# Attention and retention products as three products of halves in a hybrid encoder trunk

## The chip, the cores and the metric

The kernel runs on one core of one Trainium2 chip. The metric is the device time of one execution in microseconds, from its start to its end, here the median of several runs of the same kernel. The profile comes from one further execution, whose own time stands beside its span below.

## What is computed

The reference is a two-layer encoder trunk, applied to 16 meta tokens, 256 prompt frames and 32 frames of a running stream with 512 cached frames. The kernel puts the three side by side as 304 columns (T), with channels on the partitions, so that every dense layer is one product over 304 columns, or 288 in the second layer, where the meta columns are no longer needed (c0 = 16). What matters here, cut to its core:

```python
def retention(q, k, v, s0):              # 4 heads, 128 key and 256 value channels
    def step(s, xs):                     # chunks of 64 frames
        qc, kc, vc = xs
        att = einsum('blhk,bmhk->bhlm', qc, kc) * d_intra
        o = einsum('bhlm,bmhv->blhv', att, vc) + einsum('blhk,bhkv->blhv', qc, s) * d_q
        ...
def stick_breaking(q, k_all, v_all, q_start):    # 8 heads of 128 channels
        z = einsum('bqhd,bshd->bhqs', qblk, k_all) * scale
        log_stay = where(visible, log_sigmoid(-z), 0.0)
        later = cumsum(log_stay, axis=3, reverse=True) - log_stay
        w = where(visible, exp(log_sigmoid(z) + later), 0.0)
        return einsum('bhqs,bshd->bqhd', w, v_all)
```

A layer is: a SwiGLU feed-forward block, layer norm, one wide input product (w_in) that makes queries, keys and values of retention and attention, a pooling branch and gates, three branches merged by the gates, an output product, layer norm, a second feed-forward block and layer norm.

## The kernel before, in words

**Halves.** The dense products are not run in plain f32. Every operand x is cut into hi, which is x rounded to the type f32r by a copy on ScalarE (`act`), and lo = x - hi, also f32r, by a subtraction on VectorE; `split` (L397) does both, and `split_t` (L429) does it into two fresh buffers of 304 columns. A product is then the sum of three f32r products: hi by hi, hi by lo, lo by hi. `dense` (L359) does so for eight or 22 tiles of 128 x 128 weights in L367 to L369. The weights come from HBM in blocks of 8 tiles (512 KB) over SyncE's queue, are cut by `prep_hi` (L237) and `prep_lo` (L243), three blocks (AHEAD) before TensorE uses them, and prep_lo puts out the fetch of the block five further on (NRAW). Outside dense, retention's second product (L922 to L927) uses halves too. The scores of retention (L888 to L890), the attention's scores (L733, L734) and its prompt values (L761, L762) are plain f32 products.

**Order of the work.** The program is written out by hand: every engine runs its instructions in the order in which the code puts them out (manual_schedule). TensorE's backbone is the sequence of dense calls. Beside it, generators in the list `side` are advanced by `pump` by one step, up to their next yield, at the start of each dense call; then `tick` runs functions that were put off by `defer` for so many calls; then come the dense product's matmuls; at its end `advance` continues epilogues that are open (stages). `settle` runs all of these to their end. One dense call of eight tiles is 24 matmuls.

**Attention.** The heads are done in two groups of four (g = 0, 1). For each group, 12 dense calls make keys (ks), values (vs) and queries (qs). The first 16 of the layer's 24 calls run on un, the activations before the norm's scale is known; their epilogues (`Norm.value`, L592) correct them with VectorE and GpSimd, and a copy on ScalarE follows one call later. `v_transposes` (L702) turns the values by TensorE and copies them from PSUM into vt. Four calls after group 0's last one (in the first one after group 1's), `sb_tasks` (L1116) settles and appends the generator `sb_group` (L722) to side. Its steps: scores(0); scores(1); the running stream's scores against the cache; turn(0) and scores(2); turn(1) and scores(3); turns of the stream's weights; turn(2); the stream's values and turn(3); two more turns; values(0) and values(1); values(2) and values(3). In `scores` (L731) two products, 144 columns for the first block of 128 queries and 272 for the second, go into one PSUM bank; ScalarE takes two sigmoids of it, VectorE a scan (L740), GpSimd and VectorE products. In `turn` (L747) three transposes bring the weights of one head into PSUM and one copy brings them to wt. `values` (L758) multiplies them with vt. Group 0's generator runs beside group 1's dense calls, group 1's beside the dense calls of retention's queries and keys, whose epilogue `rotary` (L853) needs three VectorE operations a call.

**Retention.** `ret_all` (L981) starts one head, `ret_head` (L883), every two turns, beside 24 dense calls. A head's first step has its three score products and three transposes, and the VectorE work on them; the second step splits the decayed scores; the third has the products with values; the later ones the head's norm. Each of the 24 calls advances every open head by one step.

**Buffers.** Large operands of 4 x 306 columns (`newquad`, L181) share 20 buffers; buffers of 304 columns (`t304`) 16; of 576 columns (`t560`) 7; PSUM has 8 banks. A buffer is taken where its first instruction stands, and that instruction waits until the last reader of the one before is done. While the groups start, un (four large buffers, hi and lo), hn (the normed activations in halves, four more, used by the calls from the 17th on) and x (the residual, two) are in use beside the groups' own; a call of the first 16 is called a chunk, 0 to 15, so that group 1 begins with chunk 12.

Of the kernel before, what the change touches and what calls it, by code (L numbers as in the profile page):

```python
# [11 lines left out]
F32R = mybir.dt.float32r  # L12
# [11 lines left out]
T = MP + SMP  # L24
# [144 lines left out]
def trunk(ctx, tc, xT, wts, kc_d, vc_d, s0_d, sp_d, vec_d, tab_d, y_d, kv_d, ret_d, pool_d):  # L169
# [11 lines left out]
    def newquad(name, dt=F32):  # L181
        return quad.tile([128, 4, TW], dt, tag="q", name=name)
# [11 lines left out]
    def t560(name, dt=F32):  # L194
        return tmp.tile([128, 576], dt, tag="w", name=name, bufs=NT_W)

    def pa():
        return ps8.tile([128, 512], F32, tag="p", name="pa")
# [10 lines left out]
    def act(out, in_, f=AF.Copy, **kw):  # L209
        A.activation(out, in_, f, **kw)  # L210
# [96 lines left out]
    side = []  # L307
# [89 lines left out]
    def split(hi, lo, src, e=None):  # L397
        act(hi, src)
        tt(e or V, lo, src, hi.bitcast(F32), ALU.subtract)
# [33 lines left out]
        return hi, lo  # L433


    def mean(i, parts, c):
        p = pa()
        PE.matmul(p[:, c], onesr[:, i], parts[0], start=True, stop=False)
        PE.matmul(p[:, c], onesr[:, i], parts[1], start=False, stop=True)
        return p  # L440
# [256 lines left out]
    def flat(q):  # L697
        return q.rearrange("p a b -> p (a b)")
# [3 lines left out]
    def v_transposes(vs, i, vt, vm):  # L702
        p = pa()
        for k in range(4):
            o = 16 + 128 * (k % 2)
            PE.transpose(p[:, k * 128:k * 128 + 128], vs[:, i - 1 + k // 2, o:o + 128], ident)
        act(flat(vt)[:, (i - 1) * 256:(i + 1) * 256], p)
        if i == 3:
            few = t304("few")[:, 0:256]
            for k, o in enumerate((0, 272)):  # L710
                act(few[:, k * 128:k * 128 + 128].rearrange("p (a b) -> p a b", a=4), vs[:, :, o:o + 32])
            defer(3, lambda: few_transposes(few, vm))
# [9 lines left out]
    def sb_group(l, g, c0, ks, qs, kc, vc, vt, vm, oh, ol):  # L722
        meta = c0 == 0
        W = 416
        wts_t = newquad("wt")
        wt = [flat(wts_t)[:, i * 384:i * 384 + 384] for i in range(3)]
        Ys = {}
        y2 = ym[g]
        rev = lambda a: a[:, W - 1::-1]

        def scores(i):  # L731
            pz = pa()
            PE.matmul(pz[:, 0:144], qs[:, i, 16:144], ks[:, i, 0:144], start=True, stop=True)  # L733
            PE.matmul(pz[:, 144:416], qs[:, i, 144:272], ks[:, i, 0:272], start=True, stop=True)  # L734
            X, Y = t560("X"), t560("Y")
            act(X[:, 0:W], pz[:, 0:W], AF.Sigmoid, scale=-SCALE)
            act(Y[:, 0:W], pz[:, 0:W], AF.Sigmoid, scale=SCALE)
            for o in (16, 288):
                tt(G, Y[:, o:o + 128], Y[:, o:o + 128], TB("low"), ALU.mult)
            V.tensor_tensor_scan(out=rev(X), data0=rev(X), data1=rev(TB("d1p")), initial=1.0,  # L740
                                 op0=ALU.mult, op1=ALU.max)
            two = lambda a, o: a[:, o:o + 288].rearrange("p (a b) -> p a b", a=2)[:, :, 0:16]
            tt(V, y2[:, :, i, 0:16], two(Y, 0), two(X, 1), ALU.mult)
            tt(V, Y[:, 16:W - 1], Y[:, 16:W - 1], X[:, 17:W], ALU.mult)
            Ys[i] = Y

        def turn(i):  # L747
            Y = Ys.pop(i)
            p = pa()
            for k, o in enumerate((16, 160, 288)):  # L750
                PE.transpose(p[:, k * 128:k * 128 + 128], Y[:, o:o + 128], ident)  # L751
            if i == 3:
                wt.append(t560("wt3")[:, 0:384])
            act(wt[i], p[:, 0:384])

        po = []

        def values(i):  # L758
            po.append(pa())
            v = flat(vt)[:, i * 256:i * 256 + 256]  # L760
            PE.matmul(po[i][:, 0:256], v[:, 0:128], wt[i][:, 0:256], start=True, stop=False)  # L761
            PE.matmul(po[i][:, 128:256], v[:, 128:256], wt[i][:, 256:384], start=False, stop=False)  # L762

        Ws = 560 if meta else 544
        scores(0)
        yield
        scores(1)
# [115 lines left out]
    def ret_head(l, c0, h, qr, kr, vt, s0, od, var):  # L883
        vh, vl = [flat(vt[k][h // 2])[:, (h % 2) * 512:(h % 2) * 512 + 512] for k in range(2)]
        vc = flat(vt[2])[:, h * 256:h * 256 + 256]
        p, pk = pa(), pa()
        q, k = qr[:, h], kr[:, h]
        PE.matmul(p[:, c0:272], k[:, 0:128], q[:, c0:272], start=True, stop=True)  # L888
        PE.matmul(p[:, 272:416], k[:, 128:256], q[:, 128:272], start=True, stop=True)
        PE.matmul(p[:, 416:464], k[:, T - 128:T], q[:, 256:304], start=True, stop=True)  # L890
        PE.transpose(pk[:, 0:128], k[:, 0:128], ident)
        PE.transpose(pk[:, 128:256], k[:, 128:256], ident)
        PE.transpose(pk[:, 256:384], k[:, T - 128:T], ident)
# [163 lines left out]
    with tc.manual_schedule():  # L1057
# [10 lines left out]
        for l in range(DEPTH):  # L1068
# [5 lines left out]
            for g in range(2):  # L1074
                kc, vc = sb_load(l, g)
                ks, vs, qs = newquad("ks"), newquad("vs"), newquad("qs")
                vt = newquad("vt")
                vm = tmp.tile([128, 256], F32, tag="vm", name="vm")

                def k_epi(i, ks=ks, g=g):  # L1080
# [34 lines left out]

                def sb_tasks(g=g, ks=ks, qs=qs, kc=kc, vc=vc, vt=vt, vm=vm):  # L1116
                    settle()
                    side.append(sb_group(l, g, c0, ks, qs, kc, vc, vt, vm, oh[g], ol[g]))

                defer(4 - 3 * g, sb_tasks)  # L1120

# [116 lines left out]
```

## Time and profile before

| | |
|---|---|
| median of 3 runs | 1759.21 us (1758.84 to 1759.56) |
| the profiled execution's own time | 1759.8 us |
| its span | 1758.0 us |
| TensorE (PE) busy | 1748.0 us, 12736 matmuls |
| VectorE (DVE) busy | 1081.0 us |
| ScalarE (ACT) busy | 855.1 us |
| GpSimd (POOL) busy | 512.6 us |
| TensorE's granted clock | 0.999 of 2.4 GHz |

In the profile, L12 is line 12 of the kernel and pd<-hnh,whi means that the instruction writes pd and reads hnh and whi. PE's matmuls are pipelined: a row's duration holds the latency, and two matmuls overlap, so that the distance from one start to the next is the time that one takes from the engine. SP and SPq are SyncE and its queue of DMA issues. A line such as L204 or L210 is that of a helper, and the names tell which use it is. A timeline row may join several instructions of one line ("x2").

### The profile page before, as it was taken

Reading aid. Unit: us, or ns where it says so; the run is one execution under the profiler, and the core shown is the slowest. Engines: PE = TensorE matmul, PEld = TensorE weight load, DVE = VectorE, ACT = ScalarE, POOL = GpSimd, SP = SyncE. Lnnn points to the kernel's source line nnn. Section 1 sums busy time; section 2 is a strip of 40 time slices with the busy share of each in tenths; the row PEclk is TensorE's granted clock in tenths of the full one; section 3 lists DMA queues with packets and bytes.
Section 4 is the critical chain, followed back from the end, with each engine's and each line's share of the span. In section 5 each row is a group of like instructions: output and inputs, shape, how many; then the busy total and the mean of one; then the engine's idle time right before and its main releaser. Section 6 shows DMA issues by size and latency. Waiting matters only on the chain.

```text
span 1758.0 us, 31540 instructions
## 1 busy us (share of the span) xinstructions
PE 1748.0 (99%) x12736; PEld 1734.2 (99%) x12736; DVE 1081.0 (61%) x1496; ACT 855.1 (49%) x1379; POOL 512.6 (29%) x494
## 2 busy tenths in 40 slices
PE   9999999999999999999999999999999999999998
PEld 9999999999999999999999999999999999999997
DVE  5444567655785669844578445676557846796444
ACT  5444456443554446544455444475446544565442
POOL 1111336210152236411335113362101421472111
PEclk9999999999999999999999999999999999999999
DMA  7545456344345444554445544564444555446551
GB/s 286 156 156 156 156 199 218 122 149 133 119 153 181 153 148 144 172 155 160 154 140 168 157 156 156 194 230 126 153 141 127 158 183 166 147 149 189 167 166 54
DMA packets 81634, 281.18 MB, mean 160 GB/s; under 512 B 8656, under 2 KB 15440, under 8 KB 81360
## 3 DMA queue, kind: packets, MB, share of 16 engines
q1 hardware_dynamic: 80576, 276.75, 49.5%
q8 instruction: 100, 1.64, 0.4%
q0 software_dynamic: 640, 2.10, 0.3%
q14 instruction: 46, 0.38, 0.1%
q10 hardware_dynamic: 272, 0.31, 0.1%
HBM read 270.62 MB, written 8.50 MB: 159 GB/s over the span
## 4 chain that ended last, share of the span: by engine, by line
PE 99%; DMA 0%; DVE 0%; ACT 0%; issue 0%; SPq 0%; ACTq 0%
PE pd L367 30%; PE pd L368 30%; PE pd L369 30%; PE pd L387 1%; PE pd L385 1%; PE pd L386 1%; PE pa L923 0%; PE pa L734 0%; PE pa L927 0%; PE pa L761 0%; DMA raw<-in_wts 0%; PE pa L751 0%; PE pa L928 0%; PE pa L812 0%; PE pa L772 0%; PE pa L733 0%
## 5 line engine op out<-in xcount | busy, mean ns | idle before, releaser
L204 DVE TENSOR_TENSOR wlo<-raw,whi 128x1024 fp32r<-128x1024 f32 (+1 forms) x493 | 634.5, 1289 | 267.3 <-issue 140.0
L210 ACT ACTIVATE whi<-raw 128x1024 fp32r<-128x1024 f32 (+1 forms) x493 | 515.5, 1051 | 178.1 <-PE pd L368 125.3
L367 PE MATMUL pd<-hnh,whi 128*128 128x304 f32 (+1 forms) x1696 | 517.4, 305 | 0.0
L368 PE MATMUL pd<-hnl,whi 128*128 128x304 f32 (+1 forms) x1696 | 510.3, 301 | 0.0
L369 PE MATMUL pd<-hnh,wlo 128*128 128x304 f32 (+1 forms) x1696 | 509.0, 300 | 0.0
L368 PEld LDWEIGHTS pd<-hnl,whi 128*128 128x128 f32 x1696 | 320.5, 189 | 0.6
L367 PEld LDWEIGHTS pd<-hnh,whi 128*128 128x128 f32 x1696 | 319.7, 189 | 0.7
L369 PEld LDWEIGHTS pd<-hnh,wlo 128*128 128x128 f32 x1696 | 320.2, 189 | 0.0
L367 PE MATMUL pd<-sh,whi 128*128 128x304 f32 (+1 forms) x704 | 212.0, 301 | 0.0
L369 PE MATMUL pd<-sh,wlo 128*128 128x304 f32 (+1 forms) x704 | 211.9, 301 | 0.0
L368 PE MATMUL pd<-sl,whi 128*128 128x304 f32 (+1 forms) x704 | 211.9, 301 | 0.0
L204 POOL TENSOR_TENSOR sl<-sg,sh 128x304 fp32r<-128x304 f32 (+1 forms) x64 | 75.4, 1178 | 344.3 <-ACT sh L210 338.8
L367 PE MATMUL pd<-unh,whi 128*128 128x306 f32 (+1 forms) x520 | 157.5, 303 | 0.0
L368 PE MATMUL pd<-unl,whi 128*128 128x306 f32 (+1 forms) x520 | 157.1, 302 | 0.0
L369 PE MATMUL pd<-unh,wlo 128*128 128x306 f32 (+1 forms) x520 | 156.7, 301 | 0.0
L204 POOL TENSOR_TENSOR un<-un,rs_y 128x304 f32<-128x304 f32 (+1 forms) x80 | 100.2, 1260 | 146.9 <-DVE cc L595 120.5
L367 PEld LDWEIGHTS pd<-sh,whi 128*128 128x128 f32 x704 | 132.9, 189 | 0.0
L369 PEld LDWEIGHTS pd<-sh,wlo 128*128 128x128 f32 x704 | 132.8, 189 | 0.0
L368 PEld LDWEIGHTS pd<-sl,whi 128*128 128x128 f32 x704 | 132.8, 189 | 0.0
L210 ACT ACTIVATE sh<-sg 128x304 fp32r<-128x304 f32 (+1 forms) x88 | 39.9, 456 | 186.5 <-DVE sg L204 148.5
L204 DVE TENSOR_TENSOR sg<-sg,pd 128x304 f32<-128x304 f32 (+1 forms) x64 | 29.8, 466 | 122.5 <-PE pd L369 120.9
L368 PEld LDWEIGHTS pd<-unl,whi 128*128 128x128 f32 x520 | 98.3, 189 | 0.0
(286 smaller groups left out, 3160.6 us busy)
## 6 DMA issues: line engine op xcount, KB each, us to landing
raw<-in_wts SPq DMA_DIRECT2D x491, 512.0 KB, 3.6
kc<-in_kc SPq DMA_DIRECT2D x8, 512.0 KB, 5.8
vc<-in_vc SPq DMA_DIRECT2D x8, 512.0 KB, 6.8
out_kv<-ks SPq DMA_DIRECT2D x4, 608.0 KB, 5.5
out_kv<-vs SPq DMA_DIRECT2D x4, 608.0 KB, 6.0
out_ret<-st POOLq DMA_DIRECT2D x8, 256.0 KB, 2.3
tab<-in_tab SPq DMA_DIRECT2D x1, 1753.0 KB, 8.7
out_y<-x SPq DMA_DIRECT2D x4, 288.0 KB, 2.3
```

Of the source, the lines that this page charges most:

```text
L204: e.tensor_tensor(out=out, in0=a, in1=b, op=op)
L210: A.activation(out, in_, f, **kw)
L367: PE.matmul(o, wh, xh[:, c0:c1], start=(k == 0), stop=False)
L368: PE.matmul(o, wh, xl[:, c0:c1], start=False, stop=False)
L369: PE.matmul(o, wl, xh[:, c0:c1], start=False, stop=(k == n - 1))
L385: PE.matmul(o, wh, xh[:, c0:c1], start=(k == 0), stop=False)
L386: PE.matmul(o, wh, xl[:, c0:c1], start=False, stop=False)
L387: PE.matmul(o, wl, xh[:, c0:c1], start=False, stop=(k == len(xs) - 1))
```

## The change

A helper `mm3` runs a product as the three products of halves, and `cut` takes a range of columns of both halves. The attention's scores run on halves of queries and keys that `halves(i)` makes by two split_t calls: halves(0) before the generator's first yield, to which sb_tasks now advances it at once, and halves(i + 1) within scores(i), after its products. The values of the prompt (vt) and the weights (wt) become pairs: where one copy on ScalarE brought them from PSUM, split now does, with one more VectorE subtraction. The pairs take two large buffers in place of one each; the fourth head's weights take two buffers of 576 columns in place of one. In ret_head, keys and queries are split in a step of their own, ahead of the scores, so that every head has one step more. The products over cached frames, the stream's own and the meta tokens' stay as they were.

```diff
@@ -433,6 +433,15 @@
         return hi, lo
 
 
+    def mm3(out, w, x, start=True, stop=True):
+        for i, (a, b) in enumerate(((0, 0), (0, 1), (1, 0))):
+            PE.matmul(out, w[a], x[b], start=start and i == 0, stop=stop and i == 2)
+
+
+    def cut(hl, a, b):
+        return [x[:, a:b] for x in hl]
+
+
     def mean(i, parts, c):
         p = pa()
         PE.matmul(p[:, c], onesr[:, i], parts[0], start=True, stop=False)
@@ -704,7 +713,7 @@
         for k in range(4):
             o = 16 + 128 * (k % 2)
             PE.transpose(p[:, k * 128:k * 128 + 128], vs[:, i - 1 + k // 2, o:o + 128], ident)
-        act(flat(vt)[:, (i - 1) * 256:(i + 1) * 256], p)
+        split(*[flat(v)[:, (i - 1) * 256:(i + 1) * 256] for v in vt], p)
         if i == 3:
             few = t304("few")[:, 0:256]
             for k, o in enumerate((0, 272)):
@@ -722,16 +731,24 @@
     def sb_group(l, g, c0, ks, qs, kc, vc, vt, vm, oh, ol):
         meta = c0 == 0
         W = 416
-        wts_t = newquad("wt")
-        wt = [flat(wts_t)[:, i * 384:i * 384 + 384] for i in range(3)]
+        wts_t = [newquad("wth", F32R), newquad("wtl", F32R)]
+        wt = [[flat(w)[:, i * 384:i * 384 + 384] for w in wts_t] for i in range(3)]
         Ys = {}
         y2 = ym[g]
         rev = lambda a: a[:, W - 1::-1]
 
+        qk = {}
+
+        def halves(i):
+            qk[i] = split_t(qs[:, i, 16:272]), split_t(ks[:, i, 0:272])
+
         def scores(i):
+            q, k = qk.pop(i)
             pz = pa()
-            PE.matmul(pz[:, 0:144], qs[:, i, 16:144], ks[:, i, 0:144], start=True, stop=True)
-            PE.matmul(pz[:, 144:416], qs[:, i, 144:272], ks[:, i, 0:272], start=True, stop=True)
+            mm3(pz[:, 0:144], cut(q, 0, 128), cut(k, 0, 144))
+            mm3(pz[:, 144:416], cut(q, 128, 256), k)
+            if i < 3:
+                halves(i + 1)
             X, Y = t560("X"), t560("Y")
             act(X[:, 0:W], pz[:, 0:W], AF.Sigmoid, scale=-SCALE)
             act(Y[:, 0:W], pz[:, 0:W], AF.Sigmoid, scale=SCALE)
@@ -750,18 +767,20 @@
             for k, o in enumerate((16, 160, 288)):
                 PE.transpose(p[:, k * 128:k * 128 + 128], Y[:, o:o + 128], ident)
             if i == 3:
-                wt.append(t560("wt3")[:, 0:384])
-            act(wt[i], p[:, 0:384])
+                wt.append([t560(n, F32R)[:, 0:384] for n in ("wt3h", "wt3l")])
+            split(*wt[i], p[:, 0:384])
 
         po = []
 
         def values(i):
             po.append(pa())
-            v = flat(vt)[:, i * 256:i * 256 + 256]
-            PE.matmul(po[i][:, 0:256], v[:, 0:128], wt[i][:, 0:256], start=True, stop=False)
-            PE.matmul(po[i][:, 128:256], v[:, 128:256], wt[i][:, 256:384], start=False, stop=False)
+            v = [flat(x)[:, i * 256:i * 256 + 256] for x in vt]
+            mm3(po[i][:, 0:256], cut(v, 0, 128), cut(wt[i], 0, 256), stop=False)
+            mm3(po[i][:, 128:256], cut(v, 128, 256), cut(wt[i], 256, 384), start=False, stop=False)
 
         Ws = 560 if meta else 544
+        halves(0)
+        yield
         scores(0)
         yield
         scores(1)
@@ -883,11 +902,13 @@
     def ret_head(l, c0, h, qr, kr, vt, s0, od, var):
         vh, vl = [flat(vt[k][h // 2])[:, (h % 2) * 512:(h % 2) * 512 + 512] for k in range(2)]
         vc = flat(vt[2])[:, h * 256:h * 256 + 256]
+        q, k = qr[:, h], kr[:, h]
+        kh, qh = split_t(k[:, 0:T]), split_t(q[:, c0:T])
+        yield
         p, pk = pa(), pa()
-        q, k = qr[:, h], kr[:, h]
-        PE.matmul(p[:, c0:272], k[:, 0:128], q[:, c0:272], start=True, stop=True)
-        PE.matmul(p[:, 272:416], k[:, 128:256], q[:, 128:272], start=True, stop=True)
-        PE.matmul(p[:, 416:464], k[:, T - 128:T], q[:, 256:304], start=True, stop=True)
+        mm3(p[:, c0:272], cut(kh, 0, 128), cut(qh, 0, 272 - c0))
+        mm3(p[:, 272:416], cut(kh, 128, 256), cut(qh, 128 - c0, 272 - c0))
+        mm3(p[:, 416:464], cut(kh, T - 128, T), cut(qh, 256 - c0, T - c0))
         PE.transpose(pk[:, 0:128], k[:, 0:128], ident)
         PE.transpose(pk[:, 128:256], k[:, 128:256], ident)
         PE.transpose(pk[:, 256:384], k[:, T - 128:T], ident)
@@ -1074,7 +1095,7 @@
             for g in range(2):
                 kc, vc = sb_load(l, g)
                 ks, vs, qs = newquad("ks"), newquad("vs"), newquad("qs")
-                vt = newquad("vt")
+                vt = [newquad("vth", F32R), newquad("vtl", F32R)]
                 vm = tmp.tile([128, 256], F32, tag="vm", name="vm")
 
                 def k_epi(i, ks=ks, g=g):
@@ -1115,7 +1136,9 @@
 
                 def sb_tasks(g=g, ks=ks, qs=qs, kc=kc, vc=vc, vt=vt, vm=vm):
                     settle()
-                    side.append(sb_group(l, g, c0, ks, qs, kc, vc, vt, vm, oh[g], ol[g]))
+                    gen = sb_group(l, g, c0, ks, qs, kc, vc, vt, vm, oh[g], ol[g])
+                    next(gen)
+                    side.append(gen)
 
                 defer(4 - 3 * g, sb_tasks)
 
```

## Rows read from the trace of the kernel before

**Rows 1.** The page: busy time, share and instructions; chain that ended last.

```profile
PE 1748.0 (99%) x12736; PEld 1734.2 (99%) x12736; DVE 1081.0 (61%) x1496; ACT 855.1 (49%) x1379; POOL 512.6 (29%) x494
...
PE 99%; DMA 0%; DVE 0%; ACT 0%; issue 0%; SPq 0%; ACTq 0%
```

**Rows 2.** Waits of PE: waited for, us in total, times, longest.

```profile
PE pa L271 <- POOL onesr L1059: 1.1, 1, 1.1
```

**Rows 3.** PE's timeline, attention: start us, us, line, operands, shapes, xcount.

```profile
331.67 0.60 PE L761 MATMUL pa<-wt,vt 128*128 128x256 f32 x2
332.10 0.38 PE L762 MATMUL pa<-wt,vt 128*128 128x128 f32 x2
332.32 0.41 PE L733 MATMUL pa<-ks,qs 128*128 128x144 f32 x2
332.57 0.62 PE L734 MATMUL pa<-ks,qs 128*128 128x272 f32 x2
332.83 0.51 PE L367 MATMUL pd<-hnh,whi 128*128 128x304 f32 x1
333.17 0.30 PE L368 MATMUL pd<-hnl,whi 128*128 128x304 f32 x1
333.31 0.30 PE L369 MATMUL pd<-hnh,wlo 128*128 128x304 f32 x1
```

**Rows 4.** PE's timeline, scores and transposes of a retention head.

```profile
422.05 0.62 PE L888 MATMUL pa<-qr,kr 128*128 128x272 f32 x2
422.50 0.41 PE L889 MATMUL pa<-qr,kr 128*128 128x144 f32 x2
422.75 0.32 PE L890 MATMUL pa<-qr,kr 128*128 128x48 f32 x2
422.90 0.29 PE L891 MATMUL pa<-tab,kr 128*128 128x128 f32 x1
423.03 0.27 PE L892 MATMUL pa<-tab,kr 128*128 128x128 f32 x1
423.14 0.27 PE L893 MATMUL pa<-tab,kr 128*128 128x128 f32 x1
```

**Rows 5.** PE's timeline, retention: narrow f32 (L924) and wide f32r products (L927).

```profile
430.55 0.30 PE L924 MATMUL pa<-qd,s 128*128 128x32 f32 x2
430.69 0.37 PE L927 MATMUL pa<-xbh,vtrh 128*128 128x272 f32 x1
430.90 0.29 PE L927 MATMUL pa<-xbl,vtrh 128*128 128x272 f32 x1
431.02 0.29 PE L927 MATMUL pa<-xbh,vtrl 128*128 128x272 f32 x1
431.15 0.46 PE L928 MATMUL pa<-xc,vtrc 128*128 128x176 f32 x2
```

**Rows 6.** Tile st_hi: a split's copy and subtraction; ns min/median/max.

```profile
L210 ACT ACTIVATE st_hi<-rsm x8: 444/451/457, 434.2 to 1344.7; 128x304 fp32r<-128x304 f32 x4, 128x288 fp32r<-128x288 f32 x4
L204 DVE TENSOR_TENSOR st_lo<-rsm,st_hi x8: 458/468/480, 434.7 to 1345.2; 128x304 fp32r<-128x304 f32 x4, 128x288 fp32r<-128x288 f32 x4
```

**Rows 7.** ACT's timeline, last key copies before scores(0), both layers; [idle before].

```profile
286.88 0.55 ACT L210 ACTIVATE ks<-un,cc 128x304 f32<-128x304 f32 x1 [2.32 <-POOL un L204]
...
1168.17 0.55 ACT L210 ACTIVATE ks<-un,cc 128x304 f32<-128x304 f32 x1 [2.32 <-POOL un L204]
```

**Rows 8.** PE's timeline: scores(0), group 0, both layers; scores(3), group 1, first layer.

```profile
287.32 0.41 PE L733 MATMUL pa<-ks,qs 128*128 128x144 f32 x2
...
347.83 0.41 PE L733 MATMUL pa<-ks,qs 128*128 128x144 f32 x2
...
1168.23 0.41 PE L733 MATMUL pa<-ks,qs 128*128 128x144 f32 x2
```

**Rows 9.** Waits of SyncE's queue: us in total, times, longest.

```profile
SPq L693 <- DMA out_kv<-vs: 1.6, 2, 0.9
```

**Rows 10.** DVE's timeline: last rotary products ahead of group 1's third scan.

```profile
345.12 0.96 DVE L204 TENSOR_TENSOR rt<-pd,tab 64x304 f32<-64x304 f32 x2
```

## Prediction

> **What bounds the kernel now.** I read the page's busy shares and the chain that ended last first: TensorE (PE) is busy for 99% of the span and the chain is PE for 99% of it [rows 1]. The reader is to see that any PE time that a change adds or removes goes one for one into the span. Next the view of waits, for PE alone: the longest is 1.1 us, for the first constants, before the work begins [rows 2]. So in the attention and retention stages PE waits for nobody; the other engines run ahead of it and have slack, but no queue is free of order: each works through its own program, and what stands behind a late instruction is late too. Then I read PE's timeline at the products that change, since durations of pipelined matmuls overlap and only the distance of starts is a price.
>
> The sum is made against the profiled execution, 1758.0 us of span in a run of 1759.8 us; the median of the runs is 1759.21, 0.6 below it, and the forecast is the median plus the sum. About 0.2% (3.5 us) is what a measurement of this kernel can tell from no change.
>
> **Prices of the products.** A plain f32 product appears as two records. For one attention head the two score products of 144 and 272 columns cost 0.25 us (332.32 to 332.57) and 0.46 us (332.57 to the start of L368 at 333.17, less the 0.14 of the dense product between), so 0.71; the value products of 256 and 128 columns cost 0.43 and 0.22, so 0.65 [rows 3]. For one retention head L888 to L890 cost 0.45, 0.25 and 0.15, with 0.02 more between the first two transposes than between the next: 0.87 [rows 4]; the second layer has 256 columns in place of 272 there and I take 0.85.
>
> What one f32r product costs is seen only for wide ones: 272 columns start 0.125 us after one another (430.90, 431.02, 431.15) and 304 columns 0.14 [rows 3, 5], that is 0.46 ns a column: 0.118 us for 256 columns. The new products of 144, 128 and 48 columns have no row. By the column they would be 0.066, 0.059 and 0.022 us; at the price of f32 they would be 0.25, 0.22 and 0.15. The nearest row is L924 with 32 columns: from the first of its two records to the start of the second L927 are 0.35 us (430.55 to 430.90), of which the first L927 streams for 0.125, so each 32-column record took 0.11 though its columns are a quarter of that [rows 5]. I read this as the time to load 128 columns of weights, a floor that the next product, an f32r one, paid too. I take 0.112 for every f32r product under 240 columns, and keep the column price and the f32 price as ends.
>
> **The change on PE.** Each product becomes three, hi by hi, hi by lo, lo by hi. Scores, 16 heads over both layers: 3 x 0.112 + 3 x 0.125 = 0.71, as before. Values: 3 x 0.118 + 3 x 0.112 = 0.69, 0.035 more, 0.6 us in all. Retention, 8 heads: 3 x 0.125 + 6 x 0.112 = 1.05 (1.03 in the second layer), 0.175 more, 1.4 us in all. Sum on PE: **+2.0 us**.
>
> The Trainium skill ("FP8 and Floating Point Precision", TensorE Precision Notes) gives full f32 four passes through the array; three passes for four would take a quarter off the 16 x 1.36 + 8 x 0.86 = 28.6 us of these products, 7.2 us. The rows bear out the four passes for wide products (0.46 us for 272 columns against 0.125 for one f32r pass); they also show the load that narrow products don't outrun, and that turns the gain into a small loss.
>
> **The change on the other engines.** It adds to every attention head two splits ahead of the scores (256 and 272 columns) and to every retention head two of 304 or 288, each one copy on ScalarE and one subtraction on VectorE; those of 304 columns take 0.45 and 0.47 us [rows 6]. Where weights and values were copied, the copy stays and a subtraction is added. Together some 20 us on ScalarE and 35 us on VectorE. As a load PE covers that: weights are split three blocks, 10 us, ahead. What counts is who waits behind whom.
>
> First, the head start of each group. Its halves(0) is put out in the tick after settle(), and the next dense call begins with scores(0): a distance of one dense product, 3.4 us. For the first group of each layer settle() ends with a copy of keys that on ScalarE runs at 286.88, after 2.32 us of waiting for GpSimd, and for 0.55 us; in the second layer at 1168.17 [rows 7]. PE starts those scores at 287.32 and 1168.23 [rows 8]. Before, the scores didn't need that copy; now the two hi copies (0.40 and 0.42, from the 304-column price) stand behind it, and the last lo ends 0.42 later: 287.43 + 0.82 + 0.42 = 288.7 and 1170.0. PE can do the first of six products meanwhile (0.11), so it waits 1.3 and 1.65 us: 2.95. Behind the waiting VectorE subtraction stands one weight block, needed 10 us later.
>
> Added to it: the 20 large buffers. When the second group loads its caches, the four un, the four hn, one x, and the first group's two kc, two vc, ks, qs and vt are alive, 16, and the four loads make 20; the last load waits for the DMA out of the old values in both layers [rows 9]. With vt in two halves the count is 21, so a later user, the first copy of keys, must wait until the product of chunk 15 is half through (about 285.6). ScalarE loses about 3 us, of which the 2.32 us of idling give most back; I bound the cost between 0 and 0.9 us a layer and take 0.45, **+3.9 us** with the former. SyncE's queue is held up to 6 us as well, with weight fetches behind it, which are issued some 13 us before ScalarE needs them.
>
> Second, scores(3) of the second group of each layer. There VectorE also has the rotary products: it ends one at 346.08 and has the scan next, while PE reaches scores(3) at 347.83 [rows 8, 10]. Two splits added in the steps before delay it by 0.85 to 1.7 (the lower end where its waits for GpSimd absorb one), then come the lo half of the weights, 384 columns, 0.59, and those of halves(3), 0.82: done at 348.3 to 349.2. PE waits 0.4 to 1.25 us, I take 0.7 in each layer: **+1.4 us**. The first group has no rotary work beside it, and I cost its later splits at nothing; without that idle VectorE time it would pay the same 0.7.
>
> Retention: halves go out one turn, 3.4 us, ahead of the products, and later heads have the products of the head before between; nothing. The chain of the heads ends one turn later, with some six turns to spare before the drain. Its cover gone, it would cost one turn's splits, 1.8 us.
>
> Sum: 2.0 + 3.9 + 1.4 = 7.3, so 1766.5 us (1767.1 for the profiled execution's own time).
>
> **The rivals.** *Narrow f32r products cost what f32 ones do.* No row speaks for it but that none narrower than 256 columns is f32r now. Each of the three then costs 0.25, 0.22 or 0.15: 16 x (3 x 0.138 + 3 x 0.108) + 8 x (3 x 0.138 + 3 x 0.038) = 16 us more, 1782. Chance 0.14.
>
> *The waits don't come*, because ScalarE and VectorE get to the halves earlier than the keys' copy lets me think. Against it stands the program's order on ScalarE. 1761.2, within 0.2%. Chance 0.11.
>
> *The load is hidden*, so narrow products run at the column price: 48 x 0.046 + 48 x 0.053 + 24 x 0.046 + 24 x 0.09 = 8.0 us less than the forecast, 1758.5: not slower. It decides from a distance of starts under 0.086 us (8.0 us over 144 narrow products is 0.055 each; 3.8 us, which bring it within 0.2%, are 0.026 each). L924 speaks against it [rows 5]. The Trainium skill ("TensorE: Matmul & The Clock Gate", Back-to-back issue gap) gives pairs of load and matmul about 81 ns at 128 columns; by that the time would be some 4.5 us under the forecast, 1762. No row here comes that low. Chance 0.11. Both this and the former together: 1753, chance 0.04.
>
> **How the numbers follow.** Forecast 0.60, of which 0.05 ends within 0.2%; its own range is 1762 to 1770.5 (waits of 3.75 to 7.25 us, narrow products between 0.09 and 0.125). Slower by over 0.2%: 0.55 + 0.14 = 0.69. Within: 0.05 + 0.11 + 0.08 of the hidden load = 0.24. Faster: 0.04 + 0.03 = 0.07. The range 1758 to 1772 takes in all but the f32 price and the case of both, 0.18, and some 0.02 for waits that I don't see.
>
> **What would show it.** In the profile after: starts of the 144-column f32r products 0.11 us apart and of the 48-column ones too (0.02 would be the hidden load, 0.15 to 0.25 the f32 price); L734's successor, L761's and L888's totals of 0.71, 0.69 and 1.05 us a head; among PE's waits, four in all of note, two for a st_lo half at about 287.4 and 1168.3, of 1.3 to 2.2 us, and two under 1.3 us near 348 and 1227; the first copy of keys on ScalarE in the second group after, not before, the middle of chunk 15. PE waits in the retention stage, or for weights, would prove me wrong, and so would a time under 1762.

## The result, and the profile after

The changed kernel takes 1772.39 us (median of 6 runs, 1771.03 to 1773.76) against 1759.38 us for the kernel before (6 runs, 1758.64 to 1760.22): a ratio of 1.0072, 95% interval 1.0062 to 1.0083, or 13.0 us more. The forecast was 1766.5, with a range of 1758 to 1772, and the result lies 0.4 us beyond its upper end. The profiled execution, the fastest of the six, took 1771.03 us, with a span of 1769.3, 11.3 more than before.

Page of the kernel after: busy time, and the chain that ended last.

```profile
PE 1752.8 (99%) x12824; PEld 1741.1 (98%) x12824; DVE 1112.7 (63%) x1568; ACT 870.0 (49%) x1427; POOL 507.2 (29%) x494
...
PE 92%; DVE 3%; POOL 2%; ACT 1%; issue 1%; DMA 0%; SPq 0%; ACTq 0%; DVEq 0%; POOLq 0%
```

The shares of busy time hardly move, and in PE's row of the page, rounded to tenths of a slice, nothing is to be seen. The chain says it: it was PE for 99% [rows 1], and now 8% of it passes through the other engines. Waits of PE after (us in total, times, longest), which answer to [rows 2]:

```profile
PE pa L438 <- ACT st_hi L210: 4.5, 2, 2.4
PE pa L438 <- DVE st_lo L204: 2.3, 4, 1.2
PE pa L271 <- POOL onesr L1080: 1.1, 1, 1.1
```

L438 is the product in mm3. PE's timeline at three of its waits, first and second layer (idle time and what ended it in brackets):

```profile
288.73 0.33 PE L438 MATMUL pa<-st_hi 128*128 128x144 f32 x1 [2.08 <-ACT st_hi L210]
...
350.80 0.33 PE L438 MATMUL pa<-st_lo,st_hi 128*128 128x144 f32 x1 [0.67 <-DVE st_lo L204]
...
1174.82 0.34 PE L438 MATMUL pa<-st_hi 128*128 128x144 f32 x1 [2.40 <-ACT st_hi L210]
```

They stand where the prediction put them: scores(0) of the first group and scores(3) of the second. What they cost I read from the starts of the same dense products in both traces, call by call. In the first layer PE falls back by 3.0 us at scores(0) of the first group and by 0.9 at scores(3) of the second; in the second layer by 3.6 and 1.4, and by 1.3 more in the dense call behind scores(0), where no wait is listed. That is 10.2 us, and 0.57 a layer are lost in the retention's scores: with these the 11.3 us of the span are complete.

The prices of the products, in PE's timeline of the attention (answers to [rows 3]):

```profile
333.62 0.33 PE L438 MATMUL pa<-wth,vth 128*128 128x256 f32 x1
...
334.31 0.28 PE L438 MATMUL pa<-st_hi 128*128 128x144 f32 x1
334.43 0.28 PE L438 MATMUL pa<-st_lo,st_hi 128*128 128x144 f32 x1
334.55 0.27 PE L438 MATMUL pa<-st_hi,st_lo 128*128 128x144 f32 x1
334.66 0.33 PE L438 MATMUL pa<-st_hi 128*128 128x272 f32 x1
...
335.07 0.30 PE L367 MATMUL pd<-hnh,whi 128*128 128x304 f32 x1
```

and of the retention (answers to [rows 4]):

```profile
428.64 0.29 PE L438 MATMUL pa<-st_hi 128*128 128x272 f32 x1
...
429.31 0.23 PE L438 MATMUL pa<-st_hi 128*128 128x48 f32 x1
429.38 0.27 PE L438 MATMUL pa<-st_lo,st_hi 128*128 128x48 f32 x1
429.50 0.27 PE L438 MATMUL pa<-st_hi,st_lo 128*128 128x48 f32 x1
429.61 0.33 PE L912 MATMUL pa<-tab,kr 128*128 128x128 f32 x1
429.77 0.27 PE L913 MATMUL pa<-tab,kr 128*128 128x128 f32 x1
```

Products of 144 and of 48 columns start 0.11 to 0.12 us after one another; of the 0.04 by which the first two of 48 columns are closer (0.07), 0.03 come back between the first two transposes, 0.16 in place of 0.13 [rows 4]. A third of the columns take the same time, so it isn't the columns that are paid. The value products of a head take 0.69 us (333.62 to 334.31), the scores of a retention head with their first transpose 1.13 (428.64 to L913 at 429.77) against 0.98.

Why the halves come late is to be seen on the engines that make them. First layer after: PE's transposes of the first values, ScalarE's copy of them, VectorE's low half of them; then VectorE's first low half for scores(0):

```profile
258.36 0.60 PE L715 MATMUL pa<-tab,vs 128*128 128x128 f32 x4
...
263.01 0.58 ACT L210 ACTIVATE vth<-pa 128x512 fp32r<-128x512 f32 x1
...
263.62 0.69 DVE L204 TENSOR_TENSOR vtl<-pa,vth 128x512 fp32r<-128x512 f32 x1 [2.39 <-ACT vth L210]
...
288.46 0.43 DVE L204 TENSOR_TENSOR st_lo<-qs,st_hi 128x256 fp32r<-128x256 f32 x1 [1.96 <-ACT st_hi L210]
```

VectorE stands still for 2.4 us at this vtl and for 2.4 us again at the next one (271.69), since the copy that it subtracts comes late. The copy does not wait for PE, whose transposes began 4.6 us earlier: it stands in ScalarE's queue behind other work, without any idling in front of it. All the corrections of the norm are behind vtl on VectorE. ScalarE after: the first and the last copy of keys ahead of scores(0), and the high halves:

```profile
284.93 0.55 ACT L210 ACTIVATE ks<-un,cc 128x304 f32<-128x304 f32 x1 [0.39 <-PE pd L368]
...
287.50 0.55 ACT L210 ACTIVATE ks<-un,cc 128x304 f32<-128x304 f32 x1 [0.64 <-POOL un L204]
287.96 0.40 ACT L210 ACTIVATE st_hi<-qs 128x256 fp32r<-128x256 f32 x1
288.26 0.41 ACT L210 ACTIVATE st_hi<-ks 128x272 fp32r<-128x272 f32 x1
```

The last copy, at 286.88 before [rows 7], is 0.6 us later though PE runs 0.8 us ahead of the trace of before up to here (an offset that each trace takes on by its first dense calls, -1.0 to +0.5 in those of this study). And SyncE's queue, where [rows 9] had only short waits, shows the shortage of large buffers, 4.2 us at the last load of old values, once a layer:

```profile
SPq L702 <- DVE hnl L204: 8.3, 2, 4.2
```

So the mechanism that was forecast is there, at nearly twice the price. The experiments look for the rest.

### The profile page after: what moved, and what is told of

Its sections match the earlier page's. It is cut to its first block, busy times and chain, and to the rows that moved or that the text cites. A ratio compares the mean times of both kernels' runs of the same rounds, so it can differ in the third digit from the quotient of the medians.

```text
span 1769.3 us, 31802 instructions
## 1 busy us (share of the span) xinstructions
PE 1752.8 (99%) x12824; PEld 1741.1 (98%) x12824; DVE 1112.7 (63%) x1568; ACT 870.0 (49%) x1427; POOL 507.2 (29%) x494
## 4 chain that ended last, share of the span: by engine, by line
PE 92%; DVE 3%; POOL 2%; ACT 1%; issue 1%; DMA 0%; SPq 0%; ACTq 0%; DVEq 0%; POOLq 0%
PE pd L368 28%; PE pd L369 28%; PE pd L367 28%; POOL x L204 1%; PE pa L438 1%; PE pd L387 1%; PE pd L385 1%; PE pd L386 1%; DVE wlo L204 1%; POOL un L204 1%; PE pa L944 0%; DVE st_lo L204 0%; PE pa L948 0%; DVE rt L204 0%; DMA raw<-in_wts 0%
## 5 line engine op out<-in xcount | busy, mean ns | idle before, releaser
L204 POOL TENSOR_TENSOR un<-un,rs_y 128x304 f32<-128x304 f32 (+1 forms) x80 | 92.7, 1168 | 160.5 <-DVE cc L604 120.6
```

What stands on the lines that cost most here:

```text
L204: e.tensor_tensor(out=out, in0=a, in1=b, op=op)
```

## The experiments

All were timed in five rounds beside the kernel before, whose medians in them lay between 1759.20 and 1759.76 us.

**Each part alone.** In `ret_only` the kernel before gets the new lines of ret_head; in `scores_only` the scores in mm3, halves(i) and the new first yield; in `values_only` the pairs wt and vt. A line of each, in this order:

```diff
-        PE.matmul(p[:, c0:272], k[:, 0:128], q[:, c0:272], start=True, stop=True)
+        mm3(p[:, c0:272], cut(kh, 0, 128), cut(qh, 0, 272 - c0))
...
-            PE.matmul(pz[:, 0:144], qs[:, i, 16:144], ks[:, i, 0:144], start=True, stop=True)
+            mm3(pz[:, 0:144], cut(q, 0, 128), cut(k, 0, 144))
...
-        act(flat(vt)[:, (i - 1) * 256:(i + 1) * 256], p)
+        split(*[flat(v)[:, (i - 1) * 256:(i + 1) * 256] for v in vt], p)
...
```

> Before with the retention part alone (keys and queries split a step ahead, scores as three products of halves). By the theory that a narrow f32r product costs a load of 0.112 us and that nothing waits here: 8 heads x about 0.15 us = 1.2 us over before, 1760.6, with no wait of PE in that stage. If the retention's splits cost waits elsewhere (a rival: each added VectorE or ScalarE instruction delays the queues and the whole change is a load, not an order), 3 us or more.

> Before with the attention's scores alone as products of halves. By the theory of waits behind halves: PE products the same (0.1 us), the waits at scores(0) of the first group 1.3 to 2 us in each layer, since no buffer is short here, and 0.7 at scores(3) of the second: 4 to 6 us over before, 1763.5 to 1765.5. If all the loss of the change sits in the scores: 9 us or more, 1768.

> Before with only the attention's values and weights in halves. PE 0.6 us more; the large buffers are one short, so that the fourth cache load and the first key copies wait, but no PE product stands behind them: 0.6 to 1.5 us over before, 1760 to 1761. If the shortage alone costs PE time, 3 us or more.

Measured: ret_only 1760.09 us (ratio 1.0005, 0.9996 to 1.0014), scores_only 1763.14 (1.0021, 1.0013 to 1.0030), values_only 1759.62 (1.0003, 0.9994 to 1.0012): +0.9, +3.9 and +0.4 over 1759.20. The last two lie 0.4 us under what was expected of them, and the intervals of ret_only and values_only take in no change at all; that these parts cost something rests on the prices in the rows above. PE waits for halves in scores_only alone:

```profile
PE pa L438 <- DVE st_lo L204: 2.1, 4, 1.3
...
PE pa L438 <- ACT st_hi L210: 0.2, 1, 0.2
```

The parts add up to 5.2 us and the whole costs 13.0. Nearly 8 us belong to no part: the values' halves, harmless by themselves, do something to the scores' halves.

**Where the halves stand, and the buffers.** `early` puts the first group's halves(0) two dense calls earlier, ahead of the copies of keys; `late_vc` defers the second group's loads of old values by five calls, so that no buffer is short; `early_late` does both. In early, sb_first makes the generator and advances it to its first yield, and sb_tasks settles and appends it to side:

```diff
-                defer(4 - 3 * g, sb_tasks)
...
+                    defer(2, lambda box=box, f=sb_first: f(box))
+                    defer(4, lambda box=box, t=sb_tasks: t(box))
```

In late_vc, load_vc issues the two loads of vc:

```diff
-            SP.dma_start(out=vc[i].rearrange("p a b -> p (a b)")[:, 0:1024], in_=vc_d[l, 2 * g + i])
...
+        if g:
+            defer(5, load_vc)
+        else:
+            load_vc()
```

> After, with halves(0) of the first group put out two dense calls earlier, ahead of the last key copies, and the scores where they were. If the wait at scores(0) is the order of ScalarE's queue (keys' copies ahead of the halves), PE's waits of 2.8 us (first layer) and 3.4 us (second) go: about 6 us less than after, 1766. If the queues are simply too full, the wait moves to scores(1) and the time stays at 1770 or more.

> After, with the second group's two loads of cached values put off by five dense calls, so that no large buffer is short and the first copy of keys finds one free. The parts alone cost 0.9 (retention), 3.9 (scores) and 0.4 us (values), 5.2 together, the whole change 13. If the 8 us between come from the shortage (made by the values' halves, paid by the scores' halves that stand behind the keys' copies), the time falls to about 1764.5. If they come from the sheer number of splits on VectorE and ScalarE, it stays at 1771 or more.

> As late_vc, and halves(0) two calls earlier. With both hurdles gone PE waits only at scores(3) of the second group (0.9 and 1.4 us in after): 2.0 for PE's products and 2.3 of waits over before, 1763.5. If moving halves(0) only pushes the wait on to scores(1), as it did in early, no better than late_vc.

Measured: early 1772.41 us (ratio 1.0077, 1.0064 to 1.0089), late_vc 1771.76 (1.0066, 1.0053 to 1.0078), early_late 1770.02 (1.0063, 1.0049 to 1.0077). Of 13 us over the kernel before they leave 13.2, 12.2 and 10.5. Waits of PE in early:

```profile
PE pa L438 <- ACT st_hi L210: 4.3, 2, 2.3
```

With 2.3 us for st_lo the sum is nearly the old one, and the place is new: by the starts of the dense products scores(0) now loses 0.2 us and scores(1) 3.2 in the first layer and 3.5 in the second. Its halves(1) still stand behind the last copies of keys. In late_vc the loss stays at scores(0), 3.6 and 3.4 us. In all three versions PE's waits for halves are about those of the changed kernel (6.6, 6.7 and 6.5 us against 6.8), and the runs of early_late scatter from 1768.47 to 1772.74, so its 10.5 is no repair. The times are the rivals', though not every reason: that the sheer number of splits costs the time, late_vc's rival, is refuted by `ahead` below, which has them all. The shortage alone is not the cause, and neither is the place of halves(0) alone.

**One more head ahead.** `ahead` is early_late with halves(0) and halves(1) before the first yield and halves(i + 2) in scores(i).

```diff
-            if i < 3:
-                halves(i + 1)
+            if i < 2:
+                halves(i + 2)
...
+        halves(1)
```

> As early_late, with halves made two heads ahead of their scores instead of one. If all that is left are waits for halves that are put out one step ahead, none is left, and what remains is PE's own price of three products: 1.5 to 2.0 us over before, 1761. If VectorE is the limit whatever the order, 1763 or more.

Measured: 1761.13 us (1760.79 to 1761.76), ratio 1.0008 (0.9999 to 1.0016), 1.6 over the kernel before; the interval just takes in no change. PE waits for no half any more; its longest wait is again the 1.1 us for the first constants. What is left is the price of the products on PE.

**What the values do to the scores.** `vtl_late` is the changed kernel with the low half of the values one dense call later. `vtl_add` is scores_only with a subtraction behind the copy of the values that nothing needs, in a large buffer of its own. vtl_late:

```diff
-        split(*[flat(v)[:, (i - 1) * 256:(i + 1) * 256] for v in vt], p)
+        vh, vl = [flat(v)[:, (i - 1) * 256:(i + 1) * 256] for v in vt]
+        act(vh, p)
+        defer(1, lambda: tt(V, vl, p, vh.bitcast(F32), ALU.subtract))
```

vtl_add:

```diff
+        act(vh, p)
+        tt(V, flat(vtx)[:, (i - 1) * 256:(i + 1) * 256], p, vh, ALU.subtract)
```

> The changed kernel, with the low half of the values made one dense call after the copy of the high half, in place of right behind it. Theory (VectorE's queue is what makes the first group's halves late): in the profile of the changed kernel VectorE stands idle 2.4 us, at 261.2 and again at 269.3 us, because the subtraction for vtl waits for ScalarE's copy of vth, and all that is queued behind it, the norm's chain included, is about 2.3 us later at the first halves (corrections at 285.71 against 283.65 in scores_only, with starts that differ by 0.24). Put out one call later, the copy has been made and VectorE does not stand. The parts alone cost 3.9 + 0.9 + 0.4 us, so some 5 us over the kernel before, about 1764.5 us, with PE's waits for st_hi and st_lo at 2.3 us in all and the corrections back near 283.6. Rival (the added work itself, the copies and subtractions of the values and weights, or the retention halves): it stays at 1770 to 1772, with waits of 6.8 us.

> The kernel before with the attention scores on halves (scores_only), and one thing more: behind the copy of the transposed values a subtraction of 512 columns on VectorE that waits for that copy and whose result nothing reads; values, weights and retention stay plain. Theory (the wait of that subtraction is the interaction): about 8 us over scores_only, 1769 to 1771 us, with waits of PE for st_hi of 4 to 5 us and for st_lo of about 2. Rival (the weights' halves or the retention make the rest): as scores_only, 1763, or up to 1.4 us over it for the work of four subtractions.

Measured: vtl_add 1770.01 us (ratio 1.0057, 1.0044 to 1.0071), as the theory had it, 6.9 over scores_only; vtl_late 1768.99 (1.0056, 1.0043 to 1.0069), where the theory had 1764.5 and the rival 1770 to 1772: nearer the rival, with waits of 4.9 us in place of 6.8. VectorE in vtl_late does not stand at the first vtl any more, and its correction of chunk 14 (un) begins at 283.97, in scores_only at 283.90, in the changed kernel at 285.97:

```profile
264.27 0.68 DVE L204 TENSOR_TENSOR vtl<-pa,vth 128x512 fp32r<-128x512 f32 x1
...
283.97 0.53 DVE L207 SCALAR_TENSOR_TENSOR un<-lnn,cc,pd 128x304 f32<-128x304 f32 x1
288.01 0.43 DVE L204 TENSOR_TENSOR st_lo<-qs,st_hi 128x256 fp32r<-128x256 f32 x1 [3.50 <-ACT st_hi L210]
```

But now VectorE stands 3.5 us for a high half, and ScalarE shows why: its first copy of keys, which ran at 282.03 in scores_only, has to wait for a buffer until the dense product of chunk 15 lets one go.

```profile
285.22 0.55 ACT L210 ACTIVATE ks<-un,cc 128x304 f32<-128x304 f32 x1 [3.25 <-PE pd L368]
```

So I had two causes in one place, where either hides the other. vtl_add could not tell them apart, as it takes the buffer too.

**Both causes away, and one alone.** `late_both` has the edits of vtl_late and of late_vc. `short` is scores_only with a large buffer that each group holds from its first transposed values to its last product, written twice in one column by GpSimd and read by nobody.

```diff
         act(flat(vt)[:, (i - 1) * 256:(i + 1) * 256], p)
+        if i == 1:
+            G.memset(flat(vtx)[:, 0:1], 0.0)
...
         values(3)
+        G.memset(flat(vtx)[:, 0:1], 0.0)
```

> The changed kernel with both edits that did little alone: vtl one dense call later (as vtl_late) and the second group's old values loaded five calls later (as late_vc). Theory: the first halves of a layer's first group are late for either of two reasons, and each is enough alone. VectorE stands for vth (2 x 2.4 us), so the corrections of the last keys come 2.3 us later; and with one large buffer short ScalarE's first copy of keys waits for chunk 15 (in vtl_late it runs at 285.22 after 3.25 us of idling, in scores_only at 282.03 without any). With both gone the parts add up again: about 1764.5 us, PE's waits for st_hi and st_lo as in scores_only, 2.3 us in all, and the first copy of keys near 282. Rival (a third cause, such as the added load on ScalarE or the retention halves): no better than vtl_late, 1768 to 1770, with waits near 5 us.

> scores_only, with one large buffer more held by each group from its first transposed values to its last product, written by two one-column fills on GpSimd and read by nobody. It measures the shortage of buffers alone. Theory (a shortage is enough alone): ScalarE's first copy of keys after 3 us of idling near 285.2, PE's waits about 4.9 us in place of 2.3, and a time of vtl_late less the retention's and the values' share of 1.3 us: about 1767.5. Rival (the 0 to 0.9 us a layer by which the prediction bounded it): 1763 to 1765, waits of at most 4 us.

Measured: late_both 1764.99 us (ratio 1.0030, 1.0019 to 1.0042) and short 1767.23 (1.0039, 1.0025 to 1.0053), both as the theory had them; for short this is in part luck, as PE's waits are 4.4 us where 4.9 was expected, and TensorE's clock, of which the theory knew nothing, fell in its trace (below). In short the first copy of keys waits 3.22 us, in late_both not at all. First ScalarE in short, then PE's waits in late_both:

```profile
286.16 0.55 ACT L210 ACTIVATE ks<-un,cc 128x304 f32<-128x304 f32 x1 [3.22 <-PE pd L368]
```

```profile
PE pa L438 <- DVE st_lo L204: 2.2, 4, 1.1
```

Of the 13.0 us over the kernel before, vtl_late alone takes away 3.4 (9.6 are left), late_vc alone 0.8 and both together 7.8: 5.2 are left, the sum of the three parts each by itself. The 0.8 lies within the scatter of the runs. PE's waits for halves tell the same without the clock's share: 2.2 us with neither cause (late_both), 4.9 with the shortage alone (vtl_late), 6.7 with VectorE's wait alone (late_vc), 6.8 with both. The interaction is these two; by the interval of late_both (3.3 to 7.4 us over the kernel before) a third cause of more than some 2 us has no room.

**A version that beats both.** `wide` takes halves only where the product is wide: the 272 columns of the attention's scores and the first product of the retention's. The rest stays plain f32, and the halves stand as in `ahead` (its deferred loads are not needed, as values and weights are copied once).

```diff
             PE.matmul(pz[:, 0:144], qs[:, i, 16:144], ks[:, i, 0:144], start=True, stop=True)
-            PE.matmul(pz[:, 144:416], qs[:, i, 144:272], ks[:, i, 0:272], start=True, stop=True)
+            mm3(pz[:, 144:416], q, k)
...
-        PE.matmul(p[:, c0:272], k[:, 0:128], q[:, c0:272], start=True, stop=True)
+        mm3(p[:, c0:272], kh, qh)
```

> Before with products of halves only where the moving side is wide: the 272-column scores of the attention and the first product of retention (272 or 256); the products of 144, 128 and 48 columns and the values stay f32; halves(0) two calls and all halves two heads ahead. By the floor of 0.112 us for each narrow product: 16 x (0.46 - 0.375) + 8 x 0.08 = 2.0 us less than before, 1757.2, with no wait of PE. If a product of halves gains nothing when wide either, 1759 or more.

Measured: 1757.67 us (1756.72 to 1757.97), ratio 0.9987 (0.9979 to 0.9996), 1.9 under the kernel before; each of its 11 runs is below each of the 21 of the kernel before. PE's timeline of wide at one head's scores:

```profile
331.74 0.41 PE L748 MATMUL pa<-ks,qs 128*128 128x144 f32 x2
331.89 0.38 PE L438 MATMUL pa<-st_hi 128*128 128x272 f32 x1
332.11 0.29 PE L438 MATMUL pa<-st_lo,st_hi 128*128 128x272 f32 x1
332.24 0.29 PE L438 MATMUL pa<-st_hi,st_lo 128*128 128x272 f32 x1
332.37 0.30 PE L367 MATMUL pd<-hnh,whi 128*128 128x304 f32 x1
```

From 331.74 to 332.37 are 0.63 us, against 0.71 before. 16 times 0.08, and 8 times 0.45 - 3 x 0.125 = 0.075 in the retention, make 1.9.

## Why the prediction was wrong in size

**The products on PE** (+2.0): right. The floor of 0.112 us read from a 32-column f32 record [rows 5] is what the f32r products of 144, 128 and 48 columns cost. The retention came to +0.9 (1.4 forecast), the values to +0.4 (0.6), and `ahead`, which has every product of the change and no wait for a half, to +1.6. Both rivals on this price fell, f32's and the hidden load. The Trainium skill ("TensorE: Matmul & The Clock Gate", LDWEIGHTS (loading the stationary operand)) prices a load of weights at its columns over 1.2 in ns; for 128 columns that is an estimate of 107 ns. The 0.11 us of the trace agree with it, and not with the 81 ns of a pair that the section Back-to-back issue gap of the same page gives.

**Waits at scores(0)** (+2.95): the place and the order were right, the size too high. scores_only, with neither of the two disturbances, loses 0.7 and 1.1 us there, where 1.3 and 1.65 were forecast. The row that the sum was built on moved: GpSimd's correction in front of the last copy of keys starts at the same point of PE's work, but takes 0.84 us in scores_only and took 1.69 before, so that the copy comes 0.85 us earlier. First before, then scores_only:

```profile
285.15 1.69 POOL L204 TENSOR_TENSOR un<-un,rs_y 128x304 f32<-128x304 f32 x1 [1.93 <-DVE un L207]
```

```profile
284.57 0.84 POOL L204 TENSOR_TENSOR un<-un,rs_y 128x304 f32<-128x304 f32 x1 [1.93 <-DVE un L207]
```

Before, VectorE cuts weights beside it (284.93, for 1.22 us); in scores_only VectorE stands, waiting for the first high half. That this makes the difference was not tried.

**scores(3) of the second group** (+1.4): the place is right, the size 0.9 and 1.4 us, 2.3 in all. The last low half comes when I said: PE begins the scores at 349.82, 2.0 us behind the trace of before [rows 8], and goes on at 350.80, which is 348.8 there, and 348.3 to 349.2 was forecast.

**The values' split, costed at nothing** ("the copy stays and a subtraction is added [...] As a load PE covers that"): this step failed. I counted the subtraction's 0.7 us and left out its wait and what stands behind it on its engine. It is put out in the same tick as PE's transposes, VectorE gets to it before ScalarE has got to the copy, and stands until the copy is done: 2.4 us twice in each layer's first group and up to 0.9 in the second. In the first group that falls into the chunks whose corrections feed the copies of keys, and the halves behind those. The trace of before gave the bound: VectorE's work in front of this place ends at 262.06, and the copy of the transposed values, which has to be done first, at 264.41, 2.35 us later.

```profile
261.33 0.73 DVE L204 TENSOR_TENSOR hnl<-x,hnh 128x304 fp32r<-128x304 f32 x1 [1.15 <-ACT hnh L210]
...
263.83 0.58 ACT L210 ACTIVATE vt<-pa 128x512 f32<-128x512 f32 x1
```

**The buffer shortage** (+0.9 for both layers, bounds 0 to 1.8): the count of 21, the queue held at the last load, and the first copy of keys waiting for the middle of chunk 15 were right (285.22 in vtl_late against 285.6). ScalarE did lose about 3 us (3.25). The step that failed is that its idling gives most of it back: in scores_only, where GpSimd is done earlier, ScalarE has 1.47 us of idling left in front of the last copy of keys and not 2.32, and the halves come 1.6 us later (287.51 in vtl_late against 285.90). `short` costs 4.1 us over scores_only (3.5 when each is taken against the kernel before in its own rounds): PE loses 1.3 and 1.1 us more at the first scores of the two layers, and the other 1.7 are a fall of TensorE's clock behind the first of these waits. In the changed kernel the removal of the shortage alone leaves PE's waits as they were, as VectorE is late by as much. My sum should have taken the later of the two, not one plus a fraction of the other.

**TensorE's clock**, not in the prediction at all, is the remaining part. PE after, second layer, in stretches of 4 us: length, busy time (instructions), granted clock as a share of 2.4 GHz, DMA share, GB/s.

```profile
1170.00:1174.00 4.00, 2.42 (x18) 1.00 0.61 204
1174.00:1178.00 4.00, 2.96 (x13) 0.72 0.93 360
1178.00:1182.00 4.00, 4.00 (x28) 0.85 0.30 107
```

Behind the waits of 2.40 and 0.22 us the clock falls to the lower of its two levels, 1.2 GHz (the stretch from 1175.8 to 1179.2 has 0.50), and the dense products are 0.25 us apart in place of 0.14 [rows 3], 12 of them:

```profile
1176.31 0.46 PE L367 MATMUL pd<-hnh,whi 128*128 128x304 f32 x1
1176.56 0.46 PE L368 MATMUL pd<-hnl,whi 128*128 128x304 f32 x1
...
1179.10 0.36 PE L369 MATMUL pd<-hnh,wlo 128*128 128x304 f32 x1
1179.30 0.30 PE L367 MATMUL pd<-hnh,whi 128*128 128x304 f32 x1
```

This is the loss of 1.3 us in the call behind scores(0), with some 0.2 more in the scores themselves. In the first layer of the same trace, after 2.08 and 0.23 us, the clock stays at 1.00. The length of the wait does not settle it. In the first layer of `short` the clock falls behind 1.33 and 0.23 us; in the second layer of `early_late` it stays at 1.00 behind 2.25 and 0.23. PE's wait and the clock behind it (the third figure from the end; busy times of all engines stand before it), first short, then early_late:

```profile
289.21 0.33 PE L438 MATMUL pa<-st_hi 128*128 128x144 f32 x1 [1.33 <-ACT st_hi L210]
...
290.00:294.00 4.00, 4.00 (x20) 4.00 (x20) 3.90 (x6) 3.15 (x7) 2.30 (x3) 0.57 0.43 134
```

```profile
1177.94 0.34 PE L438 MATMUL pa<-st_hi 128*128 128x144 f32 x1 [2.25 <-ACT st_hi L210]
...
1178.00:1182.00 4.00, 3.77 (x26) 3.62 (x27) 3.49 (x7) 4.00 (x10) 1.37 (x3) 1.00 0.85 333
```

All traces together have 14 waits of 1.3 us or more for a high half, two in each of seven versions; behind nine of them the clock fell (after, vtl_add and short once, early, late_vc and vtl_late twice, early_late never). In the traces without such a wait it fell nowhere in the attention.

So the 13.0 us are 1.6 for PE (`ahead`), 3.6 for the waits that the parts have by themselves (5.2 less 1.6), and 7.8 for the later halves and the clock that falls behind them. The forecast had 2.0, 4.35 and 0.9 for these. Of the 7.8 the trace shows 4.5 us of longer waits at scores(0) and 1.5 of clock; the rest is the distance of the median from this run (1.4 us), for which there is no trace, and smaller terms.

## What to carry to other kernels

A product of halves pays where the columns take longer than the 0.112 us that a narrow product costs here whatever its columns: three products of 272 columns at 0.125 us beat a plain f32 one at 0.45, three of 144 at 0.112 don't beat 0.25. When a copy becomes a split, the price is not the subtraction but what its wait holds up: look at when the copy's own engine gets to it and at what is queued behind the subtraction, and put it out once the copy is done, or the halves one step further ahead. When one repair gives nothing, try it with the others before dropping it: here two edits that alone returned 3.4 us and nothing clear of the scatter returned 7.8 together.

## What was not expected of the hardware

The clock that falls behind one wait of 1.3 to 2.4 us in a kernel whose PE is busy for 99% of the span. The profile's 40 slices of 44 us don't show it, and the mean of the run shows it only in its third decimal: of the six runs of the changed kernel the three with a mean clock of 0.998 took 1771.0 to 1771.9 us and the three with 0.997 took 1772.9 to 1773.8. I read the step of about 1.8 us as one more layer in which the clock fell; the trace of late_vc shows falls in both layers (0.57 and 0.59 of 2.4 GHz over 4 us), and that of the changed kernel, a run at 0.998, in one; the other runs have no trace. The Trainium skill ("TensorE: Matmul & The Clock Gate", HAM oscillation — how this bites in real kernels) describes waits of PE for transfers that put the array back to the lower clock each time. The traces agree that a wait can do so, here one for ScalarE's copies, and show that it does not each time: nine of 14 did, one of 1.33 us among them, and two of 1.93 and 2.25 us in early_late did not. What decides between them was not tried.
